# Seven slots of split weights in place of five, with the next pieces split as a tail begins and the transposes back issued later

## The chip, the cores and the metric

The kernel runs on one core of one Trainium2 chip. The metric is the device time of one execution in microseconds, as the median of several runs. PE is the matrix engine, ACT and DVE are the scalar and the vector engine, POOL is GpSimd, and SP is the engine that issues most of the DMAs.

## The reference, cut to what matters

Two layers act on 512 tokens of width 1024, all in float32. Each layer has three sublayers, each of which ends in a layer norm, and a last step that adds a gated input embedding:

```python
for i in range(DEPTH):
    h = layer_norm(DN_ALPHA * h + 0.5 * swiglu(h, ffn_w1[i, 0], ffn_w3[i, 0], ffn_w2[i, 0]), ln_g[i, 0], ln_b[i, 0])
    ...   # layer 0: short convolution and S5 state space; layer 1: sparse attention
    h = layer_norm(DN_ALPHA * h + mix, ln_g[i, 1], ln_b[i, 1])
    h = layer_norm(DN_ALPHA * h + 0.5 * swiglu(h, ffn_w1[i, 1], ffn_w3[i, 1], ffn_w2[i, 1]), ln_g[i, 2], ln_b[i, 2])
    h = h + (p[i] @ ple_w_proj[i]) * jax.nn.sigmoid(h @ ple_w_gate[i])
```

So there are six layer norms, and almost all of the work is products with weights.

## The kernel before, in words

**Split operands.** A float32 product is made of three matmuls in a faster type: weights and activations are each split into a high part (a rounded copy) and a low part (the rest), and `mm` (L247) issues high times high, high times low and low times high. Activations lie with the features on the partitions, as `u` (float32) and the pair `x` (`xh`, `xl`).

**The stream of weights.** All weights are one list of pieces of 128x1024 values, 0.5 MB each, read in order by the class `Stream` (L53). SP loads a piece into one of three raw buffers (`wraw`), ACT copies it to the high part `whi` (L76), and an engine subtracts to get the low part `wlo` (L77); that engine is DVE, and POOL in the attention. The two parts lie in one of five slots (`wsplit`, L61). `take` hands out the next piece, and `free` gives a slot back and calls `ahead` (L101), which loads pieces up to `LOAD` = 6 and splits pieces up to `SPLIT` = 4 beyond the number that was freed. Since every engine works through its instructions in the order in which the program issues them, the place of a `free` is the place of a split in the queues of ACT and DVE.

**The tail and the norm.** Each of the six sublayers ends in `tail` (L422). It takes four pieces, then goes through four tiles of 128 tokens (t = 0 to 3), each in two halves of 512 features. For each half PE transposes what `u` holds of it into a PSUM bank (L137), adds the last four products (L438), and DVE takes the statistics (L144). After both halves `Norm.moments` (L146) computes mean and scale with 13 small DVE instructions in a row, and ACT writes the normed tile `lnt` (L167). The way back is issued later by a small planner: `tick` adds the estimated time of each PE instruction to a clock (227 ns for a matmul of 512 columns, 120 ns for one of 256), and `at` (L237) sets due times, here 4000 and 4600 ns after the moments for `back` (L169) of the two halves and 6800 and 7800 ns for `low` (L189). `back` has PE transpose four blocks (L174), ACT and DVE scale them into `u` (L182, L180), and ACT make `xh` (L184); `low` is the DVE subtraction for `xl` (L191). At t = 3 each of the four pieces is freed as soon as it was used, so `ahead` issues splits between the instructions of the last tile.

**What follows a tail.** After four of the tails (the first, second, fourth and fifth) `group` (L278) runs: four new pieces against the first 256 tokens in matmuls of 256 columns, while the last tile's way back still comes due, then a `flush` of what is due, then the other 256 tokens. After the third and the sixth tail `embed` (L1189) runs, which starts with products that do not need the normed tile. The group after the first tail is the input of the state space mixer (`mixer_ab`, L721), the one after the fourth is that of the sparse attention (`mixer_dsa`, L908), where DVE and POOL also turn the index queries and keys `qi` and `ki` (L902 to L906).

Of the kernel before, what the change touches and what calls it, by code (L numbers as in the profile page):

```python
# [52 lines left out]
class Stream:  # L53


    LOAD, SPLIT = 6, 4

    def __init__(self, nc, ctx, tc, pieces):
        self.nc, self.pieces, self.n = nc, pieces, len(pieces)
        self.raw_pool = ctx.enter_context(tc.tile_pool(name="wraw", bufs=3))  # L60
        self.pool = ctx.enter_context(tc.tile_pool(name="wsplit", bufs=5))  # L61
        self.raw, self.got = {}, {}
        self.loaded = self.split = self.used = self.freed = 0
        self.lo_engine = nc.vector
# [35 lines left out]

    def ahead(self):  # L101

        while self.loaded < min(self.n, self.freed + self.LOAD):
            self._load()
        while self.split < min(self.n, self.freed + self.SPLIT):
            self._split()

    def take(self):
        i = self.used
        while self.split <= i:  # L110
            self._split()
        self.used += 1
        return self.got.pop(i)
# [80 lines left out]
class Program:  # L194
# [83 lines left out]
    def group(self, done):  # L278

        ws = self.ws  # L280
        w = [ws.take() for _ in range(4)]
        p = [self.bank("U") for _ in range(4)]
        for h in range(2):
            cols = slice(h * HALF, (h + 1) * HALF)
            if h:
                self.flush()
            for k0 in range(0, KD, 4):
                for m in range(0, 4, 2):
                    for k in range(k0, k0 + 4):
                        for q in (m, m + 1):  # L290
                            self.mm(p[q][:, cols], w[q], self.x, [k], [k], cols, k == 0, k == KD - 1)
                    if h and k0:
                        done(m, p[m:m + 2])
                        ws.free(2)
            ws.lo_engine = self.nc.vector
            ws.SPLIT = 4

    def group_whole(self, done):

        ws = self.ws  # L300
        w = [ws.take() for _ in range(4)]
        p = [self.bank("U") for _ in range(4)]
        for k in range(KD):
            for q in range(4):
                self.mm(p[q], w[q], self.x, [k], [k], slice(0, T), k == 0, k == KD - 1)
        ws.SPLIT = 4
        for m in range(0, 4, 2):
            done(m, p[m:m + 2])
            ws.free(2)
# [112 lines left out]
    def tail(self, g, g0, ln):  # L422


        ws = self.ws
        w = [ws.take() for _ in range(4)]
        ws.SPLIT = 5
        ws.ahead()
        self.x = self.pair()
        for t in range(4):  # L430
            n = Norm(self, ln, t)
            for c in range(2):
                b = n.open()
                for k in range(TAIL):
                    gh, gl = (x[:, g0 + k, n.cols] for x in g)
                    wh, wl = (x[:, (k % 2) * T:(k % 2 + 1) * T] for x in w[2 * c + k // 2])
                    for j, (x, y) in enumerate(((gh, wh), (gh, wl), (gl, wh))):
                        self.nc.tensor.matmul(b, lhsT=x, rhs=y, start=False, stop=k == TAIL - 1 and j == 2)  # L438
                    if t == 3 and k % 2:
                        ws.free()  # L440
                    self.tick(3 * 227)
                n.stats(c)
            n.moments()
            self.at(4000, n.back, 0)
            self.at(4600, n.back, 1)
            self.at(6800, n.low, 0)
            self.at(7800, n.low, 1)
        self.pending = True


# [738 lines left out]
    def embed(self, last):  # L1189
        nc, ws = self.nc, self.ws  # L1190
        v = nc.vector
        self.lows()
        for j in range(KD):
            if j % 4 == 0:
                w = ws.take()
            b = self.bank("U")
            self.mm(b, w, self.pp_in, range((j % 4) * 2, (j % 4) * 2 + 2), range(2), slice(0, T))
            if j % 4 == 3:
                ws.free()
            nc.scalar.copy(self.pp[:, j], b)  # L1200
        self.flush()
        self.pending = False
        ws.SPLIT, ws.lo_engine = 4, v
        new = None if last else self.pair()
        banks = self.first_two(4)
        for j in range(KD):
            if j > 1:
                w = ws.take()
            if j == 4 and not last:
                ws.SPLIT = 5  # L1210
            t = self.work.tile([P, 2, T], F, name="pl", tag="t4")

            for cols in ([slice(0, HALF), slice(HALF, T)] if last and j == KD - 1 else [slice(0, T)]):
                if j < 2:
                    b = banks[j]
                else:
                    b = self.bank("U")
                    self.mm(b[:, cols], w, self.x, range(KD), range(KD), cols)
                u = self.u[:, j, cols]
                nc.scalar.activation(t[:, 0, cols], b[:, cols], AF.Sigmoid)  # L1220
                v.tensor_mul(t[:, 1, cols], t[:, 0, cols], self.pp[:, j, cols])
                v.tensor_add(u, u, t[:, 1, cols])
                if last:
                    nc.sync.dma_start(self.a["out"][:, j, cols], u)
            if j > 1:
                ws.free()
            if not last:
                self.split_pair(new, j, self.u[:, j], True)
        self.x = new
# [163 lines left out]
```

## Time and profile before

| | us |
|---|---|
| median of three runs (lowest to highest) | 2073.43 (2071.73 to 2074.17) |
| the profiled execution | 2072.32 |
| its span from the first to the last instruction | 2070.5 |
| PE busy | 1998.9 (97%) |
| DVE busy | 1064.8 (51%) |
| ACT busy | 684.4 (33%) |
| POOL busy | 94.6 (5%) |

How to read it: the span is what one profiled execution took between its first and last instruction, and the execution's own time lies 1.8 us above it. [...] An engine that is half idle can still be the one that PE waits for at some place.

### The profile page before, as it was taken

What the parts mean: (1) busy time and instruction counts of PE and PEld (TensorE: products, weight loads), DVE (VectorE), ACT (ScalarE), POOL (GpSimd) and SP (SyncE); (2) the same over time, 40 slices, a digit from 0 to 9 for tenths busy, and PEclk for the clock granted to TensorE, in tenths of its full rate; (3) what the DMA queues carried; (4) which work ended last, traced back from release to release, by engine and by line L of the source; (5) the groups of instructions that cost most, each with busy time, mean ns of one, the idle gap of its engine ahead of it and who ended that gap; (6) DMA issues with size and microseconds to landing.
All of it is one profiled execution on the core that took longest, in us unless ns stands there. A gap on an engine that the chain in (4) does not pass through costs nothing.

```text
span 2070.5 us, 24037 instructions
## 1 busy us (share of the span) xinstructions
PE 1998.9 (97%) x9550; PEld 1654.6 (80%) x9550; DVE 1064.8 (51%) x2027; ACT 684.4 (33%) x1026; POOL 94.6 (5%) x89
## 2 busy tenths in 40 slices
PE   9999999899889999998999999998999899999989
PEld 7888888787688888886888888887777788888867
DVE  5457554578554333336545554356985543333363
ACT  4223232344343222224432222233443432222242
POOL 0001110000000000000000000002431000000000
PEclk9999999999999999999999999999999999999999
DMA  5234333323213232322232322312211132323221
GB/s 204 82 103 141 122 138 106 123 96 112 99 41 123 92 102 92 103 91 72 95 104 87 107 92 92 108 56 82 82 41 61 42 122 92 102 92 103 91 72 61
DMA packets 54735, 197.99 MB, mean 96 GB/s; under 512 B 6528, under 2 KB 6816, under 8 KB 54112
## 3 DMA queue, kind: packets, MB, share of 16 engines
q1 hardware_dynamic: 51840, 187.74, 27.2%
q0 software_dynamic: 2640, 8.67, 1.2%
q8 instruction: 75, 1.23, 0.2%
q14 instruction: 36, 0.29, 0.0%
q10 hardware_dynamic: 144, 0.05, 0.0%
HBM read 187.00 MB, written 9.44 MB: 95 GB/s over the span
## 4 chain that ended last, share of the span: by engine, by line
PE 65%; DVE 7%; ACT 3%; issue 2%; DMA 1%; POOL 0%; ACTq 0%; DVEq 0%; POOLq 0%
PE U L254 44%; PE D L254 15%; PE U L438 2%; PE D L438 1%; DVE wlo L77 1%; ACT whi L76 1%; PE L L174 1%; DMA wraw<-wts 1%; PE D L1102 1%; PE U L1071 1%; PE U L137 0%; ACT lnt L167 0%; DVE zz L784 0%; ACT u L182 0%; DVE pt L1083 0%
## 5 line engine op out<-in xcount | busy, mean ns | idle before, releaser
L254 PE MATMUL U<-xh,whi 128*128 128x512 f32 (+1 forms) x2000 | 753.2, 377 | 10.1 <-ACT xh L315 5.6
L254 PE MATMUL U<-xl,whi 128*128 128x512 f32 (+1 forms) x2000 | 746.2, 373 | 5.4 <-DVE xl L322 4.1
L254 PE MATMUL U<-xh,wlo 128*128 128x512 f32 (+1 forms) x2000 | 745.5, 373 | 3.0 <-DVE wlo L77 3.0
L77 DVE TENSOR_TENSOR wlo<-wraw,whi 128x1024 fp32r<-128x1024 f32 (+1 forms) x321 | 392.7, 1231 | 326.7 <-ACT whi L76 326.5
L76 ACT CAST whi<-wraw 128x1024 fp32r<-128x1024 f32 (+1 forms) x337 | 349.6, 1044 | 570.1 <-PE D L254 272.6
L254 PEld LDWEIGHTS U<-xh,whi 128*128 128x128 f32 x2000 | 379.8, 190 | 81.4 <-ACT xh L315 7.3
L254 PEld LDWEIGHTS U<-xl,whi 128*128 128x128 f32 x2000 | 379.4, 190 | 73.6 <-DVE xl L322 6.1
L254 PEld LDWEIGHTS U<-xh,wlo 128*128 128x128 f32 x2000 | 379.2, 190 | 69.2 <-DVE wlo L77 3.8
L254 PE MATMUL D<-xh,whi 128*128 128x512 f32 x608 | 237.6, 391 | 1.4 <-DVE u L418 1.0
L254 PE MATMUL D<-xh,wlo 128*128 128x512 f32 x608 | 236.6, 389 | 0.0
L254 PE MATMUL D<-xl,whi 128*128 128x512 f32 x608 | 236.6, 389 | 0.0
L369 DVE SCALAR_TENSOR_TENSOR gt<-gt,U 128x512 f32<-128x512 f32 x88 | 60.4, 687 | 278.0 <-PE U L254 211.6
L315 ACT CAST xh<-gt 128x512 fp32r<-128x512 f32 x88 | 54.6, 620 | 384.6 <-DVE gt L369 384.6
L254 PEld LDWEIGHTS D<-xh,whi 128*128 128x128 f32 x608 | 114.1, 188 | 27.7 <-DVE u L420 3.0
L254 PEld LDWEIGHTS D<-xh,wlo 128*128 128x128 f32 x608 | 114.1, 188 | 23.9
L254 PEld LDWEIGHTS D<-xl,whi 128*128 128x128 f32 x608 | 114.1, 188 | 23.4
L420 DVE TENSOR_TENSOR u<-u,D 128x512 f32<-128x512 f32 x64 | 43.9, 686 | 112.6 <-PE D L254 112.6
L418 DVE SCALAR_TENSOR_TENSOR u<-u,D 128x512 f32<-128x512 f32 x40 | 27.4, 687 | 108.1 <-PE D L254 108.1
L174 PE MATMUL L<-ident,lnt 128*128 128x128 f32 x192 | 35.8, 322 | 32.0 <-ACT lnt L167 31.8
L322 DVE TENSOR_TENSOR xl<-gt,xh 128x512 fp32r<-128x512 f32 x88 | 60.3, 685 | 8.2 <-ACT xh L315 8.2
L368 ACT ACTIVATE gt<-U 128x512 f32<-128x512 f32 x88 | 51.6, 587 | 26.2 <-PE U L254 26.1
L174 PEld LDWEIGHTS L<-ident,lnt 128*128 128x128 f32 x192 | 24.5, 161 | 44.2 <-ACT lnt L167 43.6
(318 smaller groups left out, 1599.0 us busy)
## 6 DMA issues: line engine op xcount, KB each, us to landing
wraw<-wts SPq DMA_DIRECT2D x333, 512.0 KB, 3.5
pack<-s5d SPq DMA_DIRECT2D x4, 1792.0 KB, 10.0
s5d<-big POOLq DMA_DIRECT2D x20, 256.0 KB, 4.9
u<-x SPq DMA_DIRECT2D x8, 256.0 KB, 5.9
s5d<-big POOLq DMA_DIRECT2D x4, 512.0 KB, 3.4
out<-u SPq DMA_DIRECT2D x7, 256.0 KB, 2.0
wraw<-wts SPq DMA_DIRECT2D x4, 256.0 KB, 6.3
pt<-p POOLq DMA_DIRECT2D x2, 512.0 KB, 4.4
```

The costliest lines, as they stand in the source:

```text
L76: self.nc.scalar.copy(hi, t)
L77: self.lo_engine.tensor_sub(lo, t, hi.bitcast(F))
L174: p.nc.tensor.transpose(b[:, j * P:(j + 1) * P], self.z[:, c, j * P:(j + 1) * P], p.ident)
L254: self.nc.tensor.matmul(out, lhsT=p[:, s], rhs=q[:, xk, cols], start=first and i == 0 and j == 0, stop=last and i == n - 1 and j == 2)
L315: self.nc.scalar.copy(hi[:, j, :], src)
L322: self.nc.vector.tensor_sub(out, src, hi)
L368: nc.scalar.activation(t[:, 0], pa, AF.Silu)
L369: nc.vector.scalar_tensor_tensor(t[:, 1], t[:, 0], 0.5, pb, op0=OP.mult, op1=OP.mult)
L418: self.nc.vector.scalar_tensor_tensor(u, u, ALPHA, d, op0=OP.mult, op1=OP.add)
L420: self.nc.vector.tensor_add(u, u, d)
L438: self.nc.tensor.matmul(b, lhsT=x, rhs=y, start=False, stop=k == TAIL - 1 and j == 2)
L1071: nc.tensor.matmul(b[:, :n], lhsT=q[:, 4 * g + r, i * P:(i + 1) * P], rhs=k[:, g, :n], start=True, stop=True)
```

## The change

It does three things.

1. The ring of split slots grows from five to seven, and the distances follow it: `SPLIT` is 6 where it was 4, and loads run two pieces beyond the splits. The room comes from the program's reserve for descriptors of POOL's DMAs, which is set to 2048 bytes of a partition (`dynamic_dma_scratch_size`); before, the kernel did not set it.
2. A new method `split_to` sets the distance and splits at once. `tail` calls it with 7 as it begins and then sets the distance to 4, so that the frees of the last tile split nothing; one further piece is split in the last tile's second half, after its first products (`k == 0`). `group` and `embed` set the distance back to 6 right after their flush.
3. The transposes back are due 5000 and 5600 ns after the moments in place of 4000 and 4600, the low parts 7000 and 7600 in place of 6800 and 7800.

```diff
 class Stream:
-    LOAD, SPLIT = 6, 4
+    RING = 7
+    SPLIT = RING - 1
...
-        self.pool = ctx.enter_context(tc.tile_pool(name="wsplit", bufs=5))
+        self.pool = ctx.enter_context(tc.tile_pool(name="wsplit", bufs=self.RING))
...
-        while self.loaded < min(self.n, self.freed + self.LOAD):
+        while self.loaded < min(self.n, self.freed + self.SPLIT + 2):
             self._load()
         while self.split < min(self.n, self.freed + self.SPLIT):
             self._split()
+
+    def split_to(self, n):
+
+        self.SPLIT = n
+        self.ahead()
...
@@ group
             if h:
                 self.flush()
+                ws.split_to(ws.RING - 1)
...
-            ws.lo_engine = self.nc.vector
-            ws.SPLIT = 4
@@ group_whole
-        ws.SPLIT = 4
@@ tail
         w = [ws.take() for _ in range(4)]
-        ws.SPLIT = 5
-        ws.ahead()
+
+        ws.split_to(ws.RING)
+        ws.SPLIT = 4
...
                     if t == 3 and k % 2:
                         ws.free()
+                    if t == 3 and c and k == 0:
+                        ws.split_to(6)
+                        ws.SPLIT = 4
                     self.tick(3 * 227)
                 n.stats(c)
             n.moments()
-            self.at(4000, n.back, 0)
-            self.at(4600, n.back, 1)
-            self.at(6800, n.low, 0)
-            self.at(7800, n.low, 1)
+            self.at(5000, n.back, 0)
+            self.at(5600, n.back, 1)
+            self.at(7000, n.low, 0)
+            self.at(7600, n.low, 1)
@@ embed
-        ws.SPLIT, ws.lo_engine = 4, v
+        ws.split_to(ws.RING - 1)
...
-            if j == 4 and not last:
-                ws.SPLIT = 5
@@ kernel
-    nc = bacc.Bacc("TRN2", target_bir_lowering=False, num_devices=1)
+    nc = bacc.Bacc("TRN2", target_bir_lowering=False, num_devices=1, dynamic_dma_scratch_size=2048)
```

No engine gets an instruction more or fewer; some stand at another place in its queue. Line numbers of the changed kernel are six to eight higher than those of the kernel before (L78 for L77, L180 for L174, L186 for L180, L150 for L144).

DVE in the first tail, from the end of the moments of t = 2 to the start of those of t = 3 (`wlo` is a split, `lnst` the statistics of a half, `u` the way back of t = 2). Before:

```order
L164 SCALAR_TENSOR_TENSOR lnm<-lnmv,lny 128x1
L191 TENSOR_TENSOR xl<-u,xh 128x4x128
L77 TENSOR_TENSOR wlo<-wraw,whi 128x1024 x2
L144 BN_STATS lnst<-D 128x6
L180 TENSOR_SCALAR u<-L,lnw 128x128 x4
L77 TENSOR_TENSOR wlo<-wraw,whi 128x1024 x2
L191 TENSOR_TENSOR xl<-u,xh 128x4x128
L144 BN_STATS lnst<-D 128x6
L151 BN_AGGR lnmv<-lnst 128x2
```

And now:

```order
L170 SCALAR_TENSOR_TENSOR lnm<-lnmv,lny 128x1
L197 TENSOR_TENSOR xl<-u,xh 128x4x128
L150 BN_STATS lnst<-D 128x6
L78 TENSOR_TENSOR wlo<-wraw,whi 128x1024
L186 TENSOR_SCALAR u<-L,lnw 128x128 x4
L197 TENSOR_TENSOR xl<-u,xh 128x4x128
L150 BN_STATS lnst<-D 128x6
L157 BN_AGGR lnmv<-lnst 128x2
```

Three of the four splits between the two sets of moments have moved behind them, and the queue of ACT has moved in the same way.

PE in the group behind the first tail, around the transposes back of t = 3 (`L<-ident,lnt`), which stood in one block behind 36 matmuls of the group. Now 42 matmuls stand ahead of the first half's four transposes, and three more between the halves:

```order
L260 MATMUL U<-xh,wlo 128x256
L180 MATMUL L<-ident,lnt 128x128 x4
L260 MATMUL U<-xh,whi 128x256
L260 MATMUL U<-xl,whi 128x256
L260 MATMUL U<-xh,wlo 128x256
L180 MATMUL L<-ident,lnt 128x128 x4
L260 MATMUL U<-xh,whi 128x256
```

In the tiles t = 0 to 2 the block of eight stands six matmuls of 512 columns later than it did, and in `embed` the first four transposes stand three such matmuls later.

DVE in the group ahead of the sparse attention, between the last low part of the norm and the turn of `ki`. Before:

```order
L191 TENSOR_TENSOR xl<-u,xh 128x4x128 x2
L902 STREAM_SHUFFLE sh<-qi 128x512
L903 TENSOR_TENSOR sh<-sh,rope1s 128x512
L902 STREAM_SHUFFLE sh<-qi 128x512
L903 TENSOR_TENSOR sh<-sh,rope1s 128x512
L77 TENSOR_TENSOR wlo<-wraw,whi 128x1024
L902 STREAM_SHUFFLE sh<-qi 128x512
L903 TENSOR_TENSOR sh<-sh,rope1s 128x512
L902 STREAM_SHUFFLE sh<-qi 128x512
L903 TENSOR_TENSOR sh<-sh,rope1s 128x512
L77 TENSOR_TENSOR wlo<-wraw,whi 128x1024 x3
L902 STREAM_SHUFFLE sh<-ki 128x512
```

And now:

```order
L197 TENSOR_TENSOR xl<-u,xh 128x4x128 x2
L78 TENSOR_TENSOR wlo<-wraw,whi 128x1024 x2
L910 STREAM_SHUFFLE sh<-qi 128x512
L911 TENSOR_TENSOR sh<-sh,rope1s 128x512
L910 STREAM_SHUFFLE sh<-qi 128x512
L911 TENSOR_TENSOR sh<-sh,rope1s 128x512
L78 TENSOR_TENSOR wlo<-wraw,whi 128x1024 x2
L910 STREAM_SHUFFLE sh<-qi 128x512
L911 TENSOR_TENSOR sh<-sh,rope1s 128x512
L910 STREAM_SHUFFLE sh<-qi 128x512
L911 TENSOR_TENSOR sh<-sh,rope1s 128x512
L78 TENSOR_TENSOR wlo<-wraw,whi 128x1024 x3
```

Three splits have come in: two ahead of the first shuffle of `qi`, and one more among the turns, so that five stand where four stood between the first shuffle of `qi` and that of `ki`. In the same way five splits stand in place of four between the first copies of the group behind the first tail and the first state computation (L775).

## Rows read from the trace of the kernel before

**Rows 1.** What PE waited for, whole span: total us, times, longest us.
```profile
PE L L174 <- ACT lnt L167: 31.8, 6, 7.0
PE U L254 <- ACT whi L76: 3.4, 4, 0.8
PE U L254 <- DVE wlo L77: 3.0, 4, 0.8
PE U L267 <- DVE wlo L77: 2.2, 1, 2.2
PE L L809 <- DVE hz L796: 4.2, 2, 3.0
```

**Rows 2.** Timeline of PE, end of the first tail: start us, us, [idle before it].
```profile
386.92 0.28 PE L254 MATMUL U<-xh,whi 128*128 128x256 f32 x1
391.14 0.39 PE L254 MATMUL U<-xh,whi 128*128 128x256 f32 x1 [0.84 <-ACT whi L76]
392.40 0.39 PE L254 MATMUL U<-xh,wlo 128*128 128x256 f32 x1 [0.76 <-DVE wlo L77]
398.11 1.97 PE L174 MATMUL L<-ident,lnt 128*128 128x128 f32 x8 [4.61 <-ACT lnt L167]
```

**Rows 3.** Timeline of PE, end of the third tail.
```profile
977.01 1.11 PE L174 MATMUL L<-ident,lnt 128*128 128x128 f32 x4 [6.95 <-ACT lnt L167]
```

**Rows 4.** Busy by stretch; columns PE, PEld, DVE, ACT, POOL, granted clock, DMA share, GB/s.
```profile
398.10:402.20 4.10, 4.09 (x19) 4.10 (x20) 2.05 (x6) 3.37 (x7) 0.00 (x0) 0.50 0.96 401
977.00:982.50 5.50, 5.49 (x17) 4.62 (x18) 1.37 (x4) 4.90 (x11) 0.00 (x0) 0.50 0.01 3
514.70:517.10 2.40, 0.72 (x3) 0.30 (x2) 2.29 (x4) 2.32 (x6) 0.00 (x0) 1.00 0.07 19
1439.80:1443.20 3.40, 3.39 (x16) 3.39 (x17) 3.40 (x2) 0.85 (x2) 3.23 (x2) 0.51 0.54 167
```

**Rows 5.** Timeline of DVE, fourth tile of the first tail.
```profile
377.44 1.36 DVE L180 TENSOR_SCALAR u<-L,lnw 128x128 f32<-128x128 f32 x4 [1.02 <-PE L L174]
385.26 2.36 DVE L77 TENSOR_TENSOR wlo<-wraw,whi 128x1024 fp32r<-128x1024 f32 x2 [1.85 <-ACT whi L76]
388.14 1.35 DVE L180 TENSOR_SCALAR u<-L,lnw 128x128 f32<-128x128 f32 x4
391.12 2.36 DVE L77 TENSOR_TENSOR wlo<-wraw,whi 128x1024 fp32r<-128x1024 f32 x2 [1.63 <-ACT whi L76]
393.40 0.68 DVE L191 TENSOR_TENSOR xl<-u,xh 128x512 fp32r<-128x512 f32 x1
394.00 0.69 DVE L144 BATCH_NORM_STATS2 lnst<-D 128x6 f32<-128x512 f32 x1
```

**Rows 6.** Timeline of ACT, the same stretch.
```profile
382.84 1.45 ACT L167 ACTIVATE lnt<-U,lnm,lny 128x512 f32<-128x512 f32 x2 [3.39 <-DVE lnm L164]
384.18 1.99 ACT L76 CAST whi<-wraw 128x1024 fp32r<-128x1024 f32 x2
397.28 1.45 ACT L167 ACTIVATE lnt<-D,lnm,lny 128x512 f32<-128x512 f32 x2 [5.24 <-DVE lnm L164]
```

**Rows 7.** Timeline of DVE, ahead of the sparse attention.
```profile
1431.83 2.32 DVE L77 TENSOR_TENSOR wlo<-wraw,whi 128x1024 fp32r<-128x1024 f32 x1
1437.48 6.72 DVE L77 TENSOR_TENSOR wlo<-wraw,whi 128x1024 fp32r<-128x1024 f32 x3
1446.23 0.69 DVE L906 TENSOR_TENSOR ki<-sh 128x512 f32<-128x512 f32 x1
```

**Rows 8.** Timeline of PE, the first product on ki.
```profile
1447.02 0.45 PE L960 MATMUL D<-ki,qi 64*128 64x256 f32 x1 [0.91 <-issue]
```

**Rows 9.** Timeline of ACT, after the group behind the first tail.
```profile
426.09 1.05 ACT L76 CAST whi<-wraw 128x1024 fp32r<-128x1024 f32 x1 [1.99 <-DMA wraw<-wts]
```

**Rows 10.** Timeline of POOL, setup of the state-space weights.
```profile
180.99 3.73 POOL L618 DMA_DIRECT2D s5d<-big  x7 [6.89 <-DVE big L608]
```

**Rows 11.** DMA issues: KB each, median us to landing.
```profile
s5d<-big POOLq DMA_DIRECT2D x20, 256.0 KB, 4.9
```

## The prediction

> **What bounds the kernel now.** PE is busy for 97% of the span, so a gain can only come from where it waits or runs at the lower clock. I read the list of what PE waited for first. One line leads it: 31.8 us in six waits of the transposes back for `lnt`, the normed tile; beside it stand 3.4 us for `whi` and 3.0 us for `wlo`, four waits each [rows 1]. Six is the number of tails, four the number of groups. PE's timeline shows the place [rows 2]: the group behind the first tail starts at 386.92, halts 0.84 us for a high part and 0.76 us for a low part, then 4.61 us for `lnt` of the last tile. In `embed` there is only the long wait, 6.95 us [rows 3]. The sum of the idle time is 31.8 + 3.4 + 3.0 = 38.2 us.
>
> The waits cost more than their idle time. [...] Half of such a stretch is lost: 2.05 us in each of four groups and 2.75 us in each of two `embed`s, 13.7 us. All six tails together lose **51.9 us**, and that is all that this change can win.
>
> Why `lnt` is late is read from the timelines of DVE and ACT in the last tile [rows 5, 6]. `lnt` of t = 2 starts at 382.84. Then DVE stands 1.85 us until ACT has cut a piece, splits two pieces (2.36 us), takes one set of statistics, runs the way back of t = 2 (1.35 us), stands 1.63 us for ACT again, splits two more (2.36 us) and only then, at 394.00, takes the last statistics; `lnt` of t = 3 follows at 397.28. The four splits and the standing before them, 8.2 us, lie in the chain that PE waits for.
>
> **The change part by part.**
>
> *Splits out of the chain.* One of the four splits stays between the two sets of moments. I go through the new order with durations of these rows, after shifting the start for the moved transposes. In tiles 0 to 2 these come six matmuls of 512 columns later, by the program's own 227 ns 1.37 us. DVE already stands 1.02 us for them before its way back [rows 5], and its next statistics stand behind that, so the whole shift reaches the next moments. It does not add up over tiles: the next moments end early enough for the next block, which is later by as much. So `lnt` of t = 2 starts at 382.84 + 1.37 = 384.2. DVE has the next low part (0.68) and statistics (0.69) done at 385.5. ACT is free at 385.6 and starts one `whi`; in the rows `wlo` starts 1.08 us after the start of its `whi` (385.26 less 384.18 [rows 5, 6]), so at 386.6. Split 1.2, way back 1.35, low part 0.68: 389.8. Statistics start there, and `lnt` follows 3.28 us later as before (397.28 less 394.00): **393.1, 4.2 us earlier**.
>
> *Transposes back later.* PE began them 0.83 us after `lnt` (398.11 less 397.28); that is now 393.9. PE gets there from 386.9 by 42 matmuls of 256 columns in place of 36; at the program's 120 ns that is 392.0 if no weights are late. They are not: three pieces are ready before the last tile, and the fourth is split by 387.8 and needed first by the 25th matmul, at 389.8. So 1.9 us are left of 6.2. In `embed` PE used to arrive at 977.01 - 6.95 = 970.06; three matmuls later is 970.7, `lnt` lets it go 4.2 us earlier, at 972.8, and 2.1 us are left.
>
> *The clock after what is left.* Two rows bound it. After the wait of 2.2 us for a low part at 1437.6 [rows 1] PE ran 3.40 us at 0.51, which loses 1.7 us; after one of 1.7 us the clock stayed at 1.00 [rows 4]. The 2.1 us of `embed` are nearest to the first, so I take 1.7 us there; the 1.9 us of a group lie between, so I take half, 0.85. What is left is 4 x (1.9 + 0.85) + 2 x (2.1 + 1.7) = 18.6 us, and the gain in the tails 51.9 - 18.6 = **33.3 us**. [...]
>
> *More splits behind the tails.* Behind the fourth tail DVE has five splits in place of four before the turn of `ki`. In that stretch it works without a break, and PE waits for `ki`: DVE's last step on it starts at 1446.23 and takes 0.69 us [rows 7], and PE's product on it starts at 1447.02 [rows 8]. So the 2.2 us wait for a low part [rows 1], which the larger ring removes, wins nothing, and the fifth split delays `ki` by its own length. Splits here take 2.32 us, and 6.72 for three [rows 7], against 1.18 elsewhere [rows 5]; they run beside POOL's part of the turn. The bounds are 1.2 and 2.3 us, and I take 2.2, since its neighbours are these. PE then stands idle for the 0.9 us of now [rows 8], the 2.2 and 1.7 us that its vanished wait and slow stretch no longer fill, and the new 2.2: 7 us, and the clock falls. Of the 2.75 us that this costs after 6.95 us [rows 4] I take 1.0, since PE's first matmuls there wait for ACT anyway. That is -3.2 us, with bounds of 0 and -5. [...]
>
> Behind the first tail the state computation on DVE also has one more split before it, and PE waits for its result (4.2 us in two waits for `hz` [rows 1]). Since only three raw buffers exist, the last of a burst waits for its load, as one does now for 1.99 us [rows 9]. I take one split of 1.2 us: **-1.2 us**, between 0 and -3.
>
> *Edits that cost nothing.* At the start two more loads and two splits stand ahead of the state-space setup on SP and DVE; PE waits for neither [rows 1], and two free banks cover the later first gate, without which the setup's delay of some us would show once. In steady work the distance from a split to the slot that it reuses is what it was. The smaller descriptor reserve touches only POOL's DMAs, which are issued at 3.73 us for seven [rows 10] with much time to spare; its bad case is a rival.
>
> *The sum.* 33.3 - 3.2 - 1.2 = 28.9 us from the profiled execution's 2072.3 gives 2043.4. The median of the runs is 1.1 us above that execution, so **2044.5**, rounded to 2044.
>
> **The rivals.**
>
> *Nothing is left to wait for* (0.12). If the moments come 2 us sooner than in my walk, for which the short 1.02 us of standing would have to shrink, the tails lose nothing: 51.9 - 4.4 = 47.5 us, 2026.
>
> *Every restart is slow* (0.10). A wait of 1.9 us may count like one of 2.2 us. Then each of four groups loses 0.85 us more, 3.4 us in all: 2048. For it speaks the stretch at 0.51, against it the one at 1.00 [rows 4]. [...]
>
> *The later transposes drag the moments* (0.08). DVE runs the way back of one tile ahead of the statistics of the next. If the 1.37 us add up over three tiles, `lnt` comes 2.7 us later than I have it. Then 4.6 us are left in a group and 4.8 us in `embed`, with about 2.05 and 2.4 us of slow clock: 4 x 6.65 + 2 x 7.2 = 41.0. The gain is 10.9 - 4.4 = 6.5 us, 2067. For it speaks that standing [rows 5], against it that each block moves by as much as its tile.
>
> *Slower: POOL's descriptors* (0.05). The setup sends two bursts of eight DMAs of 256 KB from POOL, issued 0.53 us apart [rows 10] and landing after 4.9 us [rows 11]. If the reserve of 2048 bytes holds one of them at a time, seven issues of a burst wait some 4.4 us each, 30.6 us, with memsets behind them on POOL that DVE needs next; DVE in turn stands ahead of splits and gates. PE has two products, 48 matmuls of 227 ns or 10.9 us, before it lacks banks, so a burst costs up to 19.7 us and two cost 39.4: 2084. It turns the result once a burst is delayed by more than 10.9 + 14.5 = 25.4 us, so six of seven issues must wait. Nothing in the trace speaks for it: the issues follow without a gap. The trace cannot show the smaller reserve.
>
> *No difference* (0.03). Three raw buffers still feed the ring. If the early pieces were not loaded in time, the splits would slide back into the last tile and the time would stay at 2073. Against it: only one piece is split as the tail begins, and it was loaded before.
>
> **How the numbers follow.** My case has 0.62: DVE's queue in the last tile is plain in the trace, and only sizes are estimates. Its own range is 2027 to 2058, from a residue 1 us shorter without a slow clock and no loss behind the tails (6 x 1 + 6.8 + 4.4 = 17 us better) to one 1 us longer with the larger losses and all restarts slow (6 + 3.6 + 3.4 = 13 us worse). It holds the case of slow restarts. For 8 in 10 the range takes in the time of the first rival and leaves out those of the drag, the descriptors and no difference, which have 0.16 between them: **2026 to 2058**. A measurement of this kernel tells about 0.2%, 4 us, from no change. Faster by more than that: 0.62 + 0.10 + 0.12 + 0.08 = 0.92; within it 0.03; slower 0.05.
>
> **What would show it.** In the waits of PE the lines for `whi` and `wlo` behind a tail are gone, and that for `lnt` falls from 31.8 to about 12 us in six waits. DVE shows one `wlo` between the two sets of moments of the last tile, and `lnt` follows the start of the group by 6 us, not 10.4. PE's wait for `ki` grows from 0.9 to some 7 us. The forecast is wrong if the wait for `lnt` stays above 4 us in a group, if it is gone altogether, or if POOL's bursts in the setup stretch from 4 to over 20 us.

## The result and the profile after

The changed kernel takes **2035.71 us** (2035.43 to 2036.14, 4 runs), the kernel before 2073.44 (2071.73 to 2074.17, 4 runs): a ratio of 0.9819, with a 95% interval of 0.9802 to 0.9836. The forecast was 2044, between 2026 and 2058. The profiled execution took 2035.52 us, with a span of 2033.8, 36.7 us less than before.

What PE waited for, whole span of the changed kernel (total us, times, longest us):

```profile
PE L L180 <- ACT lnt L173: 9.3, 7, 1.7
...
PE D L968 <- issue: 4.8, 1, 4.8
...
PE D L777 <- DVE m L786: 2.6, 1, 2.6
PE D L777 <- issue: 2.0, 1, 2.0
PE L L817 <- DVE hz L804: 1.4, 1, 1.4
...
PE L L952 <- ACT wt L945: 1.4, 1, 1.4
PE D L777 <- DMA pack<-s5d: 1.3, 1, 1.3
...
PE U L260 <- ACT pp L1208: 1.2, 2, 0.6
```

Against [rows 1] the wait for `lnt` has fallen from 31.8 to 9.3 us, and the lines for `whi` and `wlo` are gone. Six lines are new or longer. The product on `ki` (L968, the "issue" line, for which the profile names no releaser) waits 4.8 us, and the transposes ahead of it 1.4 us for `wt`. The state-space products (L777) wait 2.6, 2.0 and 1.3 us. In `embed`, matmuls wait 1.2 us in two halts for `pp`, the copy that frees their bank. The wait for `hz`, the result of the state computation, falls from 4.2 to 1.4 us.

The end of the first tail, then of the third, on PE (start us, us, and in brackets the idle time before):

```profile
392.76 0.66 PE L180 MATMUL L<-ident,lnt 128*128 128x128 f32 x4 [1.66 <-ACT lnt L173]
...
960.07 1.32 PE L180 MATMUL L<-ident,lnt 128*128 128x128 f32 x8 [1.22 <-ACT lnt L173]
...
966.20 0.50 PE L260 MATMUL U<-ph,whi 128*128 128x512 f32 x1 [0.61 <-ACT pp L1208]
```

They answer to [rows 2, 3]: 1.66 us in place of 0.84 + 0.76 + 4.61, and 1.22 + 0.61 in place of 6.95. Four transposes behind the wait take 0.66 us, and in `embed` eight take 1.32; before, eight took 1.97 and in `embed` four 1.11. The granted clock of the stretches shows the same. Busy time by stretch (us, PE busy, granted clock, DMA share, GB/s), behind two of the waits for `lnt` and behind three of the others:

```profile
392.70:395.40 2.70, 2.64 (x23) 1.00 0.03 6
427.10:432.00 4.90, 4.84 (x23) 0.65 0.00 0
...
476.20:480.40 4.20, 4.14 (x19) 0.59 0.00 0
960.00:962.40 2.40, 2.31 (x13) 1.00 0.00 0
...
1422.10:1427.00 4.90, 4.83 (x27) 0.69 0.17 70
```

Where [rows 4] had 0.50 behind the first and the third tail, the granted clock is now 1.00; the stretches behind the other four tails have 1.00 too. Behind two waits in the state space and the one for `ki`, its mean is 0.65, 0.59 and 0.69.

The fourth tile of the first tail on DVE, and ACT's two `lnt`, those of t = 2 and t = 3:

```profile
385.63 1.23 DVE L78 TENSOR_TENSOR wlo<-wraw,whi 128x1024 fp32r<-128x1024 f32 x1 [1.24 <-ACT whi L77]
...
388.66 0.69 DVE L150 BATCH_NORM_STATS2 lnst<-D 128x6 f32<-128x512 f32 x1
```

```profile
383.22 1.45 ACT L173 ACTIVATE lnt<-U,lnm,lny 128x512 f32<-128x512 f32 x2 [3.39 <-DVE lnm L170]
...
391.93 1.44 ACT L173 ACTIVATE lnt<-D,lnm,lny 128x512 f32<-128x512 f32 x2 [3.14 <-DVE lnm L170]
```

One split of 1.23 us is left where [rows 5] had four, and the last statistics start at 388.66 in place of 394.00.

To see where the time went, take one instruction in both traces behind each stage (a PE matmul, behind the second tail an ACT instruction) and follow its shift:

| behind | before, us | after, us | shift | the stage itself |
|---|---|---|---|---|
| start of the program | 19.75 | 18.88 | -0.87 | -0.9 |
| first tail | 403.29 | 395.36 | -7.93 | -7.1 |
| state space | 544.51 | 539.32 | -5.20 | +2.7 |
| second tail (start of a gate's ACT work) | 617.52 | 605.00 | -12.52 | -7.3 |
| third tail, `embed` | 990.25 | 970.65 | -19.60 | -7.1 |
| fourth tail | 1414.47 | 1388.22 | -26.25 | -6.7 |
| sparse attention | 1590.07 | 1566.51 | -23.55 | +2.7 |
| fifth tail | 1639.94 | 1609.89 | -30.05 | -6.5 |
| sixth tail, `embed` | 2025.71 | 1988.99 | -36.72 | -6.7 |

The six tails give 41.3 us, and the two stages behind the first and the fourth of them take back 5.4. The 0.9 us of the start is no part of the change: the matmul of the first line starts between 18.6 and 20.4 us in the profiled executions of all the kernels here, and at 18.8 in the kernel before with nothing but more slots.

### The profile page after: what moved, and what is told of

The parts are those of the page before. It is cut to its first block, busy times and chain, and to the rows that moved or that the text cites. A ratio compares the mean times of both kernels' runs of the same rounds, so it can differ in the third digit from the quotient of the medians.

```text
span 2033.8 us, 23989 instructions
## 1 busy us (share of the span) xinstructions
PE 1986.0 (98%) x9550; PEld 1645.0 (81%) x9550; DVE 1066.5 (52%) x2027; ACT 684.1 (34%) x1026; POOL 94.3 (5%) x89
## 3 DMA queue, kind: packets, MB, share of 16 engines
q8 instruction: 75, 1.23, 0.3%
## 4 chain that ended last, share of the span: by engine, by line
PE 64%; DVE 8%; ACT 4%; issue 2%; POOL 0%; DMA 0%; DVEq 0%; ACTq 0%; POOLq 0%
PE U L260 44%; PE D L260 15%; PE D L443 1%; PE U L443 1%; DVE wlo L78 1%; ACT u L188 1%; ACT whi L77 1%; PE D L1110 1%; ACT lnt L173 1%; PE U L1079 1%; DVE xl L197 0%; DVE lnst L150 0%; PE L L180 0%; ACT xh L190 0%; DVE zz L792 0%
## 5 line engine op out<-in xcount | busy, mean ns | idle before, releaser
L78 DVE TENSOR_TENSOR wlo<-wraw,whi 128x1024 fp32r<-128x1024 f32 (+1 forms) x321 | 393.6, 1232 | 303.3 <-ACT whi L77 301.8
L77 ACT CAST whi<-wraw 128x1024 fp32r<-128x1024 f32 (+1 forms) x337 | 350.6, 1045 | 559.7 <-PE D L260 309.3
L186 DVE TENSOR_SCALAR u<-L,lnw 128x128 f32<-128x128 f32 x96 | 32.8, 404 | 32.6 <-PE L L180 32.6
L173 ACT ACTIVATE lnt<-D,lnm,lny 128x512 f32<-128x512 f32 x24 | 17.4, 773 | 72.3 <-DVE lnm L170 72.3
```

Of the source, the lines that this page charges most:

```text
L77: self.nc.scalar.copy(hi, t)
L78: self.lo_engine.tensor_sub(lo, t, hi.bitcast(F))
L173: p.nc.scalar.activation(self.z[:, c], self.banks[c], AF.Identity, bias=m, scale=y)
L186: p.nc.vector.tensor_scalar(out, x, gam, bet, op0=OP.mult, op1=OP.add)
```

## Experiments

The theory was that the splits inside DVE's last tile were what PE waited for, and that the due times only shift PE against DVE. The first four kernels take the change apart. Each ratio is against the kernel before on the same chip (median there 2071.83 us, 27 runs; for the later groups of kernels 2073.02 and 2071.84, 9 runs each). The changed kernel ran beside a median of 2073.44, so medians of kernels from different groups compare only to some 1.6 us; where a difference is smaller, the traces decide.

**The slots and the reserve alone.** The kernel before with

```diff
-        self.pool = ctx.enter_context(tc.tile_pool(name="wsplit", bufs=5))
+        self.pool = ctx.enter_context(tc.tile_pool(name="wsplit", bufs=7))
...
-    nc = bacc.Bacc("TRN2", target_bir_lowering=False, num_devices=1)
+    nc = bacc.Bacc("TRN2", target_bir_lowering=False, num_devices=1, dynamic_dma_scratch_size=2048)
```

> The kernel before with seven slots and the reserve of 2048 bytes, nothing else: no piece is split earlier, no transpose moves. Theory (the gain comes from what DVE does in the last tile): 2073.4 us, within 2 us, and PE's waits for lnt stay at 31.8 us in six. Rival of the descriptor reserve: POOL's bursts in the setup stretch and the time goes up, to 2084 by the sum on record. A rival by which the free slots alone help: below 2069.

Measured: 2071.78 us, ratio 1.0000 (0.9991 to 1.0009). PE's waits, against [rows 1]:

```profile
PE L L174 <- ACT lnt L167: 31.9, 6, 7.0
```

The halts for `whi` and `wlo` are as before too (3.4 and 3.0 us). The slots only make room, and the reserve costs nothing here.

**The due times alone.** The kernel before with 5000, 5600, 7000 and 7600.

> The kernel before with the later due times alone; the splits stay in the last tile. By the walk lnt comes 1.37 us later and PE arrives 0.72 us later in a group (six matmuls of 120 ns) and 0.68 in embed (three of 227), so each wait grows by 0.65 us: 2073.4 + 6 x 0.65 = 2077. If lnt does not follow the moved transposes at all, each wait shrinks by 0.7 us: 2069. If the shift adds up over the tiles to 2.7 us (the drag), each wait grows by 2 us: 2085.

Measured: 2075.85 us, ratio 1.0019 (1.0010 to 1.0028): slower, by 4 us. PE's wait for `lnt`, and ACT's `lnt` of t = 3 in the first tail:

```profile
PE L L174 <- ACT lnt L167: 41.6, 7, 7.0
```

```profile
398.27 1.45 ACT L167 ACTIVATE lnt<-D,lnm,lny 128x512 f32<-128x512 f32 x2 [5.05 <-DVE lnm L164]
```

Most of the halts for `whi` and `wlo` have gone into the one wait, six times 6.9 us. All idle time of the tails, 42.6 us with 1.0 us for `wlo` in short halts, is 4.4 us above the 38.2 of before. `lnt` of t = 3 starts at 398.27, 11.7 us behind the start of the group (386.53), where it was 10.4: 1.4 us later, as in the walk. So half of the change, taken alone, costs time: PE comes 0.7 us later, and `lnt` 1.4. The shift does not add up as in the drag.

**The splits without the due times.** The changed kernel with 4000, 4600, 6800 and 7800.

> The changed kernel with the due times of before; splits and slots as in the changed kernel. By the walk lnt comes 1.37 us earlier than in the changed kernel (391.9 in the first tail, so 390.6) while PE arrives 0.7 us earlier: what is left falls from 1.66 to 1.0 us in a group and from 1.2 to 0.5 in embed, and the time is 2035.7 - 6 x 0.65 = 2032. Rival, lnt is bound by the split that stays between the moments and not by the transposes: lnt stays, what is left grows to 2.4 and 1.9 us, the time is 2035.7 + 4.3 = 2040, and 2050 if the clock then falls for 3.4 us at each restart.

Measured: **2032.27 us**, ratio 0.9810 (0.9797 to 0.9824), 3.4 us below the changed kernel's median on another chip. The first tail's `lnt` of t = 3 on ACT, and PE's transposes on it:

```profile
390.49 1.45 ACT L173 ACTIVATE lnt<-D,lnm,lny 128x512 f32<-128x512 f32 x2 [3.14 <-DVE lnm L170]
```

```profile
391.32 1.32 PE L180 MATMUL L<-ident,lnt 128*128 128x128 f32 x8 [1.01 <-ACT lnt L173]
```

`lnt` is 1.44 us earlier than in the changed kernel (391.93), the wait 1.01 us, and both are what the walk through DVE's order gives. The ratios of the two kernels overlap, but the traces tell them apart: PE's waits for `lnt` and `pp` fall from 10.5 to 6.5 us, and by the shift of PE's matmuls the six tails are 3.5 us shorter. The whole gain is the splits'; the due times of the change cost some 3 us of it. In `embed` 1.2 us are left in either kernel, since there PE and `lnt` both move by about 1.4 us.

**The due times and slots without the earlier splits.** In the tail of the changed kernel:

```diff
-        ws.split_to(ws.RING)
-        ws.SPLIT = 4
+        ws.split_to(5)
...
-                    if t == 3 and c and k == 0:
-                        ws.split_to(6)
-                        ws.SPLIT = 4
```

> The changed kernel with its seven slots, its reserve and its due times, but the four splits back in the last tile (one piece ahead at the start of a tail, one with each slot that comes free). Theory (the splits in DVE's chain are what PE waited for): lnt follows the start of a group by about 10 us again in place of 6, the waits of PE come back to some 6 us in all six tails, the clock falls at the restart, and the time is 2035.7 + 51.9 - 10.3 (idle that is left in the changed kernel) - 4.3 (later transposes) = 2073, between 2064 and 2079. Rival (slots or due times alone made the gain): 2036 to 2042.

Measured: 2072.94 us, ratio 1.0007 (0.9999 to 1.0016). Three splits stand in the last tile here, since two pieces are ahead by then. PE's waits, then busy time by stretch behind the first and the third tail (PE, PEld, DVE, ACT, POOL, granted clock, DMA share, GB/s):

```profile
PE L L180 <- ACT lnt L173: 36.9, 7, 6.4
```

```profile
397.01:401.10 4.09, 4.09 (x20) 4.09 (x21) 1.44 (x5) 2.78 (x7) 0.00 (x0) 0.53 1.01 419
976.24:981.70 5.46, 5.46 (x18) 4.69 (x19) 1.36 (x4) 5.43 (x11) 0.00 (x0) 0.55 0.01 3
```

Long waits, the lower clock and the old time are back. With slots and due times as in the changed kernel, only the place of the splits makes the difference.

**The clock behind waits of six lengths.** The forecast had put half or all of a slow stretch behind waits of 1.9 and 2.1 us; there is none. One kernel tries six lengths, one in each tail:

```diff
-            self.at(5000, n.back, 0)
-            self.at(5600, n.back, 1)
+            at = {0: 4600, 1: 4300, 2: 4700, 3: 3900, 4: 3550, 5: 4000}[ln] if t == 3 else 5000
+            self.at(at, n.back, 0)
+            self.at(at + 600, n.back, 1)
```

> The changed kernel with other due times for the transposes back of tile 3, a different one in each tail, so that PE arrives earlier by steps of three matmuls. Expected waits for lnt, in the order of the tails: 2.0 and 2.4 us (groups), 1.9 us (embed), 2.7 and 3.1 us (groups), 2.6 us (embed). The waits add 5.6 us. If the length of the wait decides on the clock, as the rows of before have it (1.7 us: 1.00; 2.2 us: 0.51), the stretches behind 2.4, 2.7, 3.1 and 2.6 us run at the lower level, some 1.7 to 2 us lost at each: 2048 us. If the restart is not slowed by the wait's length alone, but by the short halts for weights ahead of it that the changed kernel no longer has, all six restart at full clock: 2041 us. The step between the two levels, if there is one, is read from the windows behind the six waits.

Measured: 2043.43 us in one run. The six waits, and the stretches behind them (us, PE busy, granted clock, DMA share, GB/s):

```profile
394.27 0.66 PE L180 MATMUL L<-ident,lnt 128*128 128x128 f32 x4 [2.03 <-ACT lnt L173]
...
589.82 0.66 PE L180 MATMUL L<-ident,lnt 128*128 128x128 f32 x4 [2.37 <-ACT lnt L173]
...
961.47 0.66 PE L180 MATMUL L<-ident,lnt 128*128 128x128 f32 x4 [1.91 <-ACT lnt L173]
...
1386.64 0.66 PE L180 MATMUL L<-ident,lnt 128*128 128x128 f32 x4 [2.74 <-ACT lnt L173]
...
1611.57 0.66 PE L180 MATMUL L<-ident,lnt 128*128 128x128 f32 x4 [3.16 <-ACT lnt L173]
...
1985.47 0.65 PE L180 MATMUL L<-ident,lnt 128*128 128x128 f32 x4 [2.60 <-ACT lnt L173]
```

```profile
394.30:400.00 5.70, 5.70 (x49) 1.00 0.01 3
589.90:595.50 5.60, 5.60 (x48) 1.00 0.00 0
961.50:966.50 5.00, 5.00 (x26) 1.00 0.01 3
1386.70:1392.30 5.60, 5.60 (x35) 0.70 0.02 4
1611.60:1617.20 5.60, 5.60 (x35) 0.70 0.00 0
1985.50:1990.50 5.00, 5.00 (x26) 1.00 0.00 0
```

Behind the four waits up to 2.60 us the clock stays at 1.00. Behind 2.74 and 3.16 us the mean over 5.6 us is 0.70, which loses 5.6 x 0.30 = 1.7 us each. The first four transposes take 0.65 or 0.66 us in all six, so in the two slow ones the fall comes only after the restart. The sum comes near: 5.7 us more waiting (15.0 less 9.3) and 3.4 us of slow clock, less 1.0 us of the wait for `pp`, which shrinks as PE comes earlier to the transposes, make 2035.5 + 8.1 = 2043.6. That is luck in part: by the shifts the six tails are 6.8 us longer, and 1.5 us of the rest is a later start of the program. Length alone does not tell them apart: the clock was 0.51 behind a wait of 2.20 us in the kernel before [rows 1, 4], and 0.65 and 0.59 behind waits of 2.6 and 2.0 us at L777 in the changed one (the stretches at 427.10 and 476.20), but 1.00 behind 2.37 and 2.60 us here. What PE did just before does not tell them apart either: ahead of the waits of 2.20 and 2.0 us it was busy at 1.00 (1432.0 to 1437.5 before, 464.0 to 474.2 after), as in the tails. And each wait was seen in one execution; no run shows whether the same wait ends the same way each time.

**One split fewer behind the tails.** The other price that the forecast had put on the change:

```diff
                         done(m, p[m:m + 2])
+                        ws.SPLIT -= less * (m > 0)
                         ws.free(2)
...
         self.turn(ki, v)
+        ws.SPLIT = ws.RING - 1
```

with `less` = 1 in the state-space and the sparse-attention stage and 0 elsewhere, and the same return to six behind the first state computation.

> The changed kernel with one split fewer behind the first and the fourth tail before the state computation and the turn of ki, so four in each place as in the kernel before. Theory (the added split is what these stages lose, 2.7 us each in the two traces): most of it comes back, some 2 us at each place: 2035.7 - 4 = 2031.7 us, between 2030.3 and 2033.7, and PE's wait for ki falls from 4.8 us to about 2.9. Rival: the split is needed there, PE waits for a low part again as in the kernel before (2.2 us, and the clock falls): 2035 to 2039.

Measured: 2036.03 us, ratio 0.9821 (0.9808 to 0.9835), that is no gain: the rival's time, with other waits than it named. These are this kernel's first product behind `ut` and first product on `ki`, then its waits for `hz`, then the stretch behind the longer of these:

```profile
425.14 2.02 PE L778 MATMUL D<-ut,pack 128*128 128x128 f32 x16 [0.59 <-DVE m L787]
...
1420.51 0.76 PE L972 MATMUL D<-ki,qi 64*128 64x256 f32 x1 [5.14 <-issue]
```

```profile
PE L L818 <- DVE hz L805: 5.4, 2, 4.2
```

```profile
450.60:456.00 5.40, 5.34 (x23) 0.50 0.51 174
```

The first wait shrinks by 2.0 us (2.59 to 0.59), so the added split did delay that product. But PE is then early for `hz`, which DVE computes: that wait grows from 1.4 to 4.2 us, and the clock falls to 0.50 behind it. At `ki` the product comes 1.1 us earlier against the work before it, a later wait for `relu` takes 0.9 us back (2.2 in place of 1.3), and the clock behind the two waits is lower (0.51 from 1420.5 to 1425.5, 0.62 from 1434.5 to 1439.0). By the shift of PE's matmuls the state space gains 0.5 us on the changed kernel, and the sparse attention loses 1.8. A split taken from one wait came back in the next, with a slow stretch behind it.

**Later due times for tile 3 alone.** Two versions of this edit, in which `LATER` and `OTHERS` stand for four due times each:

```diff
+            for ns, f, c in zip(LATER if t == 3 else OTHERS,
+                                (n.back, n.back, n.low, n.low), (0, 1, 0, 1)):
+                self.at(ns, f, c)
```

The first has the due times of before (4000, 4600, 6800, 7800) for tiles 0 to 2, and 5700, 6300, 7700, 8300 for tile 3.

> The changed kernel with the due times of before for tiles 0 to 2, and for tile 3 alone later ones (5700, 6300, 7700, 8300). Theory: lnt comes as early as with the old due times, PE arrives 1.2 us or more later than there, so that the waits of 1.0 us in four groups and 1.2 us in two embeds, 6.4 us in all, are gone: 2032.3 - 6.4 = 2025.9 us. Rival: the way back is then late for the second half of the columns, and PE waits there for xl or xh of tile 3: 2030 us or more.

Measured: **2025.96 us** (2025.54 to 2026.09), ratio 0.9773 (0.9759 to 0.9786). PE waits for `lnt` nowhere. One small wait in `embed` has grown (0.6 to 1.0 us each, twice):

```profile
PE U L260 <- ACT pp L1207: 2.0, 2, 1.0
```

The second has the changed kernel's due times for tiles 0 to 2, and 6700, 7300, 8700, 9300 for tile 3.

> The changed kernel with its due times for tiles 0 to 2 kept, and for tile 3 later ones alone (6700, 7300, 8700, 9300), so that PE arrives at the transposes of tile 3 some 1.7 us later in a group and 2 us later in embed. If PE's arrival is all that the due times change while lnt stays where it is, the waits of 1.66 and 1.22 us are gone: 2035.7 - 4 x 1.66 - 2 x 1.22 = 2026.6 us, the same as with the due times of before for tiles 0 to 2 (2026.0), since an lnt that nobody waits for may come 1.4 us later. Rival: with the later lnt and later transposes the way back of tile 3 reaches the second half of the columns too late: 2029 or more.

Measured: 2030.12 us, ratio 0.9800 (0.9787 to 0.9814). The rival's time, but not its mechanism: the groups don't wait for `lnt` any more, and `embed` waits elsewhere. The waits of PE, and ACT ahead of the first of the two:

```profile
PE U L260 <- ACT pp L1207: 4.7, 2, 2.4
```

```profile
955.65 1.45 ACT L173 ACTIVATE lnt<-D,lnm,lny 128x512 f32<-128x512 f32 x2 [3.14 <-DVE lnm L170]
956.99 1.56 ACT L1207 COPY pp<-U 128x512 f32<-128x512 f32 x3
```

The copies of `pp`, which free PE's banks, stand behind `lnt` in ACT's order, and ACT stands 3.14 us for the moments. With PE's own wait for `lnt` put off, PE runs out of banks: 2.4 us twice in place of 1.22 + 0.61. From the changed kernel that is 2035.7 - 4 x 1.66 + 2 x (2.37 - 1.83) = 2030.1. An `lnt` that is 1.4 us earlier is thus worth something although PE no longer waits for it by name.

**The state space's splits on POOL.** The version of 2025.96 us with

```diff
             if m == 0:
                 along(0)
+                ws.lo_engine = nc.gpsimd
...
             f(i)
+        ws.lo_engine = v
         self.lows()
```

> The best version so far (2026.0 us: due times of before for tiles 0 to 2, later ones for tile 3) with the low parts of the state space stage cut by POOL in place of DVE, from behind the first two turned streams to the product of the gates. Theory: in that stage DVE sets the time (one split fewer ahead of the first product only moved its wait to the next), so that taking some twelve splits of 1.22 us off DVE brings back the 2.7 us that the changed kernel lost there and part of the 5.6 us that PE stood there before: 2019 to 2023 us. Rival: POOL's splits (2.40 us each where the trace has them, beside DVE's 1.22) hold up DVE's own work on tensors in SBUF, or come too late for PE: 2026 us or more.

Measured: 2024.31 us, ratio 0.9772 (0.9758 to 0.9785): between the theory and the rival, and by the ratios not to be told from the version without POOL (0.9773). The groups of DVE between 405 and 535 us (busy us, mean ns, idle before) without POOL, then with it, and PE's longest wait with it:

```profile
L791 DVE TENSOR_TENSOR_SCAN zz<-s5r,zz 128x128 f32<-128x128 f32 x32 | 10.5, 402 | 0.0
...
L787 DVE TENSOR_TENSOR zz<-m 128x512 f32<-128x512 f32 x4 | 2.8, 692 | 0.1
...
L782 DVE TENSOR_TENSOR m<-D,pack 128x512 f32<-128x512 f32 x4 | 2.8, 688 | 0.1
```

```profile
L792 DVE TENSOR_TENSOR_SCAN zz<-s5r,zz 128x128 f32<-128x128 f32 x32 | 17.0, 603 | 0.0
...
L788 DVE TENSOR_TENSOR zz<-m 128x512 f32<-128x512 f32 x4 | 4.5, 1136 | 0.1
...
L783 DVE TENSOR_TENSOR m<-D,pack 128x512 f32<-128x512 f32 x4 | 2.8, 688 | 5.3 <-PE D L777 5.2
```

```profile
PE L L817 <- DVE hz L804: 8.9, 2, 6.1
```

Both were right in part. The waits at L777 are gone, and by the shift of PE's matmuls the stage is 2.0 us shorter; but DVE's own work on SBUF tensors stretches, the scan from 402 to 603 ns, and the wait for `hz` reaches 6.1 us. The means of `zz<-m` go from 692 to 1136 ns, and those of the copies `ut<-us`, which have one input, in SBUF, from 217 to 352 ns, while the product with one input in PSUM (`m<-D,pack`) stays at 688 ns, and `vv<-uu,small,vv`, without PSUM, at 752 (751 with POOL). What decides which of them stretch is not shown.

**Both at once.** The version of 2025.96 us with one split fewer behind the tails.

> Both: due times of before for tiles 0 to 2 and later ones for tile 3, and one split fewer behind the first and the fourth tail. If the two gains are in different stages and add up: 2025.9 - 4 = 2022 us. If they share one wait (the time won in a tail is lost again at the state computation or at ki, where DVE and not PE sets the time): 2025 us.

Measured: 2027.24 us (2025.61 to 2028.71), ratio 0.9778 (0.9765 to 0.9791): the split fewer gains nothing here either.

## Why the prediction was right, point by point

The direction and the mechanism were right: the splits left DVE's chain, and PE's wait for `lnt` went with them. The forecast of 2044 (2044.5 before rounding) was 8.8 us too high: the tails gave 8.0 us more than forecast, the two stages behind them took 1.0 more (1.5 more in one, 0.5 less in the other), the start was 0.9 earlier, and the profiled execution lay 0.2 us below the median in place of 1.1.

- *Splits out of the chain.* Forecast: `lnt` of t = 3 at 393.1, 6.2 us behind the start of the group. Measured: 391.93, with the group starting at 385.90, 6.03 us. Right to 0.2 us. That the moved transposes make it later by 1.37 us is shown by the kernel with the old due times, where it comes 1.44 us earlier.
- *Transposes back later.* In a group, forecast: 1.9 us left. Measured: 1.66. In `embed` the step "three matmuls later" failed, as did the same count in the account of the change: PE ran 24 in place of 18 before the first four transposes (953.22 to 958.85 us, before 965.82 to 970.06), six more; three is what the second four moved. So 1.22 us were left in place of 2.1, and a halt of 0.61 us for `pp`, which the forecast did not have, came behind it.
- *The clock after what is left.* For the kernel before, the forecast counted half of 4.10 us as lost in each group and half of 5.50 us in each `embed`, from the two stretches at 0.50 in [rows 4]; stretches as long behind the second, fourth, fifth and sixth tail have 0.50, 0.61, 0.62 and 0.59 there. What it left of this loss is the step that failed: 0.85 us in each group and 1.7 us in each `embed`, 6.8 us in all. No restart in the tails was slow, and in the kernel with six lengths none was up to 2.60 us. The forecast leaned on one row at 0.51 behind 2.2 us, in another stage, for waits in the tails. The row at 1.00 behind 1.7 us was the one that held for the 1.66 us that came.
- *More splits behind the fourth tail.* Forecast: -3.2 us. Measured: -2.7 us. The place was right. DVE's five splits end at 1419.4, and `ki` follows:

```profile
1405.57 4.54 DVE L78 TENSOR_TENSOR wlo<-wraw,whi 128x1024 fp32r<-128x1024 f32 x2
...
1413.73 5.65 DVE L78 TENSOR_TENSOR wlo<-wraw,whi 128x1024 fp32r<-128x1024 f32 x3
...
1421.38 0.69 DVE L914 TENSOR_TENSOR ki<-sh 128x512 f32<-128x512 f32 x1
```

  They take 10.2 us where four took 9.0 [rows 7]. PE stands 1.4 us for `wt` and 4.8 for `ki`, 6.2 in place of the "some 7"; its product on `ki` starts at 1422.17, when DVE's last step on it is done. Both parts of the term were off, in opposite directions: by PE's shift that product comes 1.4 us later, not 2.2 (without the fifth split, 1.1 us of it goes), and what follows it, with the slow stretch, takes 1.3, not 1.0. That the sum came within 0.5 us is in part luck.
- *Behind the first tail.* Forecast: -1.2 us, between 0 and -3. Measured: -2.7, and not at the wait that the forecast named. The wait for `hz` did not grow; it fell from 4.2 to 1.4 us, and the slow stretch behind it (0.50 from 457.3 to 462.8 before) is gone (1.00 from 451.4 to 454.7). What grew are the waits at the first products of the state computation, 5.9 us in all where the kernel before had

```profile
PE D L769 <- PE U L254: 0.9, 1, 0.9
PE D L769 <- DVE m L778: 0.5, 1, 0.5
```

  and two of the restarts there are slow (0.65 and 0.59). The added split delays the first product on the second stream by 2.0 us: its own 1.2, and 0.8 in which DVE stands for it, since ACT waits 0.96 us for its load. But without it the stage still loses 2.2 us (its end lies 0.5 us earlier), so one split is not the whole cause: another of the stage's restarts is slow there (0.50 from 450.6 to 456.0).
- *Edits that cost nothing.* Right: slots and reserve alone changed nothing, and POOL's bursts of DMAs take 3.73 us as before [rows 10].
- *The rivals.* "Nothing is left to wait for" was wrong for this change, with 9.3 us left, but its time is that of the version with later due times for tile 3 alone. "Every restart is slow" fell. "The later transposes drag the moments" fell: `lnt` of t = 3 comes 1.4 us later, as in the forecast, and not 2.7. The descriptors cost nothing.

One thing is open: why the clock falls behind some waits (0.51 behind 2.20 us) and not behind others (1.00 behind 2.60 us). Of the 2.2 us that the state-space stage loses even with one split fewer, PE's shifts put 1.2 on the longer wait for `hz` (4.2 us, before 3.0) and most of the rest on a slow stretch at the end of the stage, behind waits that are the same in both kernels (4.9 and 2.0 us), which lasts longer (0.50 from 519.0 to 523.5 in the changed kernel, from 524.8 to 528.4 before).

## What to carry to other kernels

When a small engine's chain ends in a wait of the big one, list everything that stands in its queue between the last input and the result, and move out what others could have had earlier; here three of four splits of 1.2 us, moved in each of six places, were worth some 40 us, and the room for them cost nothing. Set a due time for the instance that is waited for, and not for all of its kind: with the splits moved, later due times cost some 3 us when every tile had them, and gained some 6 when the last alone had them (with 1700 units in place of 1000). Price a wait behind a moved one too, and test halves of a change by themselves, since one of them may work against the other.

## What the runs showed that was not expected

- PE's granted clock stayed at 1.00 behind waits of 1.9, 2.0, 2.4 and 2.6 us in the tails, but not behind 2.7 and 3.2 (a mean of 0.70 for each), and elsewhere it fell behind 2.0, 2.2 and 2.6 us (0.59, 0.51 and 0.65).
- Behind 2.7 and 3.2 us it fell only after the restart: the first four transposes take 0.66 us behind 3.16 us of waiting as behind 1.66. Behind the 4.6 us of before they were slow at once (1.97 us for eight, which take 1.32 in `embed` now).
- One step of the due times counts differently by stage: a thousand units put the first transposes behind six more matmuls in a group (0.12 us apart in the trace), and behind six more in `embed` (0.23 us apart).
